# RWKV-7 hybrid block on one core: the product with the keys' norms ordered behind the fourth chunk's state update, with other places for the RWKV matmuls, the branch inputs and the output projection's first rounding

## The chip, the cores and the metric

The kernel runs on one core of a Trainium2 chip. A core has a matrix engine, TensorE (PE in the profile, its weight loads PEld), a vector engine (DVE), an activation engine (ACT), GpSimd (POOL) and SyncE (SP), whose work here is to issue DMA transfers. Each engine takes its instructions in an order fixed at compile time, and they wait for each other through semaphores. The metric is the device time of one execution in microseconds (us).

## What is computed

One decoder residual block over 512 positions of width 2048, in float32: an RWKV-7 time mixer and a sliding-window attention in parallel, both gated, projected and added to the input, then a gated convolutional feed-forward net.

```python
h = rms_norm(x, norm1_g);  z = h @ w_in
zs = token_shift(z[..., :RW_SHIFT_COLS], rw_mu)          # r, k, v and the low-rank inputs
o_rw  = rwkv7_mix(zs, ...);  o_att = swa_attention(q, k, v, ...)
g_rw, g_att = sigmoid(zg[..., :D_MODEL]), sigmoid(zg[..., D_MODEL:])
x = x + (g_rw * (o_rw @ w_branch[:RW_DIM]) + g_att * (o_att @ w_branch[RW_DIM:])) @ w_out
x = x + conv_ffn(rms_norm(x, norm2_g), w_up, conv_w, conv_b, w_down)
```

Inside the time mixer, with 16 heads of 64 channels:

```python
kk = k * k_k
kk = kk / max(sqrt(sum(kk * kk, per head)), 1e-12)        # the keys' norms
k  = k * (1 + (a - 1) * k_a)
# per position t:
sa    = state @ (-kk_t)
state = state * w_t + sa (x) (kk_t * a_t) + v_t (x) k_t
y_t   = state @ r_t
```

## The kernel before

**Precision.** Each float32 operand is split into a rounded high part (float32r, made on ACT) and a bfloat16 rest (made on DVE: value less high part); a product is three matmuls, high x high, high x low and low x high. `load_w` does this for a weight tile of 128 x 512: a DMA on SP's queue into `raw` (4 buffers), `whi` on ACT (L263), `wlo` on DVE (L264). `project` then issues 12 matmuls for each such tile (L284) and appends them to a list, `stream`.

**The stages.** Input projections for attention; the attention; the RWKV stage, in which the input projections of the gates run along; the branch projections (`w_branch`, again L284); the output projection `w_out` (L1107) and the feed-forward net (L1244, then L1107), each as a fast product of seven block products.

**The RWKV stage.** 16 heads are eight pairs `p`. `early(p)` projects k, r and v of the pair (three tiles of 48 matmuls), forms the decays and the keys' norms; `late(p)` does the recurrence in eight chunks of 64 positions. In the loop, `late(p)` is written down first, then a gate projection, `early(p + 1)`, and two more gate projections: six tiles, 288 stream matmuls for a pair. Pair `p` begins at stream index `base` = 960 + 288 p. So while the chunks of pair p run, the keys' norms of pair p + 1 are made.

**The keys' norms.** In `early`: `sq` on ACT (L642), sums on PE (L396), a reciprocal root of 13 small DVE instructions (`rq`, L198 to L207), and then `head_rows`: a transpose on PE (L399), a copy `rsT` on DVE (L401), a DMA from it to DRAM (`rsd`, L403) and two DMAs back that broadcast it over partitions (`rsb`, L407), all three on SP's queue. The product `kk = kk * rb` (L683, on DVE, kept in program order with the other instructions marked by `pin`) waits for them. Behind it come `kb = kk * ta` (L684, written into the tile `kz`), `bon` (L689, which doesn't need kk), and in the next `late` `BKK` (L699 from kb, L700 from k2) and `BAR` (L701 from kk, L702 from r), the operands of the first products L719.

**A chunk of `late`.** psG on PE (L848), GY on ACT (L851), psU on PE (L853), UV half on ACT (L855) and half on DVE (L856), psS on PE (L864), the state update SV of two DVE instructions (L870), then the next chunk's psG. After the fourth and the eighth chunk two DVE additions make `yc` (L876).

**What sets the order.** A scheduler at compile time orders the instructions of each engine by the order of writing and its own estimates, within the edges that the program gives. `behind(ins, before)` adds such an edge: `ins` is placed after `before`. It is an order, not a semaphore. With `held`, 34 or 35 matmuls of each pair are placed behind given stream matmuls: `entries` (the transposes, the levels of the triangular inverse, psG, psU and psS of the chunks) behind stream index `base + n + lag - 1`, n from the lists `LEVEL` and `CHUNK`. For psS of the eight chunks n is 175, 189, 203, 221, 235, 249, 263 and 277; a chunk's psU is four before it, its psG five before that (the first psG has no place). The transpose L399 has no such place.

**After the pairs.** `rin[i]` reads back the eight pairs' outputs from DRAM, and `split(rhi[:, i], ...)` rounds them on ACT and DVE for the branch projections; the last gate projections are written down between these roundings. Then `wp["step"]` and other counters set how often extra DRAM-to-DRAM sums are issued; they are not touched. In the output projection, `steps_of("o", i, ...)` fetches a tile `hraw` of the right operand and rounds it with `make()` (hhi on ACT, hlo on DVE, in `split`, L216 and L217); the first two are written after the branch projections but have buffers of their own, so the scheduler may place them earlier.

Of the kernel before, what the change touches and what calls it, by code (L numbers as in the profile page):

```python
# [13 lines left out]
AF = mybir.ActivationFunctionType  # L14
ALU = mybir.AluOpType
# [4 lines left out]
P = 128  # L20
S = 512
NT = S // P
# [113 lines left out]
def block_kernel(ctx: ExitStack, tc: tile.TileContext, d: Dims, a: dict, out: bass.AP):  # L136
    nc = tc.nc
    act, dve, pool, pe, sync = nc.scalar, nc.vector, nc.gpsimd, nc.tensor, nc.sync
    NK, NP, NQ, NKV, NF = d.NK, d.NP, d.NQ, d.NKV, d.NF
# [73 lines left out]
        return ins  # L213

    def split(hi, lo, src, pin=free):
        pin(act.activation(hi, src, AF.Copy))  # L216
        pin(dve.tensor_tensor(lo, src, hi.bitcast(F32) if hi.dtype == F32R else hi, op=ALU.subtract))  # L217


    def quarter(w, src, c):  # L220
# [31 lines left out]
    def behind(ins, before):  # L252
        tc.add_manual_dep(ins.ins, before.ins.name,
                          mybir.DependencyInfo(mybir.DependencyClass.NoSync, mybir.DependencyReason.DATA))

    def load_w(src):
        nk, ncol = src.shape[1:]
        n = nk * ncol
        raw = wp["raw"].tile([P, 512], F32, name="raw", tag="raw")[:, :n].rearrange("p (k c) -> p k c", c=ncol)
        wp["last"] = sync.dma_start(raw, src)  # L260
        hi = wp["hl"].tile([P, 512], F32R, name="whi", tag="whi")[:, :n].rearrange("p (k c) -> p k c", c=ncol)
        lo = wp["hl"].tile([P, 512], BF16, name="wlo", tag="wlo")[:, :n].rearrange("p (k c) -> p k c", c=ncol)
        act.activation(hi, raw, AF.Copy)  # L263
        dve.tensor_tensor(lo, raw, hi.bitcast(F32), op=ALU.subtract)  # L264
        wp["n"] += 1
        if wp["n"] in wp["after"]:
            wp["after"].pop(wp["n"])()
        elif wp["step"] == 3 and wp["n"] <= HELD:
            pass
        elif wp["n"] % wp["step"] == 0 or wp["n"] in extra:  # L270
            sums_along()()
        return hi, lo
# [23 lines left out]
    if True:  # L296
# [99 lines left out]
                pe.matmul(dst[:, t], sq[:, t * P : (t + 1) * P], K["sel2"], start=True, stop=True)  # L396

        def head_rows(pl, ps, rs, tag="lg", bufs=1):
            pe.transpose(ps[0 : 2 * NT, 0:P], rs, ident)  # L399
            sm = pl.tile([2 * NT, P], F32, name="rsT", tag="rsT", bufs=2)  # L400
            dve.tensor_copy(sm, ps[0 : 2 * NT, 0:P])  # L401
            rd = dram.tile([2 * NT, P], F32, name="rsd", tag="rsd", bufs=4)
            sync.dma_start(rd, sm)  # L403
            rb = pl.tile([P, S], F32, name="rsb", tag=tag, bufs=bufs)
            src = rd.rearrange("(h t) c -> h (t c)", h=2)
            for h in range(2):
                sync.dma_start(rb[h * HD : (h + 1) * HD], src[h : h + 1].to_broadcast([HD, S]))  # L407
            return rb
# [151 lines left out]
        with ExitStack() as pr:  # L560
# [21 lines left out]
            def bulk():  # L582
                return blk.tile([P, S], F32, name="bulk", tag="bulk")
# [41 lines left out]
            def r3(ap, c=C):  # L625
                return ap.rearrange("p (n c) -> p n c", c=c)

            def early(p):
                wl = lp.tile([P, 2 + NG, P], F32, name="wl", tag="wl", bufs=1)
                sync.dma_start(wl, a["lora"][p].rearrange("p (k c) -> p k c", c=P))  # L630
                w2 = wl[:, 0]
                ag = [lp.tile([P, NG, P], F32R, name=f"w{e}", tag=f"w{e}", bufs=2) for e in ("ghi", "glo")]
                split(*ag, wl[:, 2:])

                sums_along(up_jobs)()
                acc = ztile(d.c_k + p * P)
                kz = wtile("kz")
                shifted(acc, PR["mu"] + NP + p, kz, 0)
                kk = wtile("kk")
                dve.tensor_scalar(kk, kz, col("k_k", p), None, op0=ALU.mult)  # L640
                sq = wtile("lg")
                act.activation(sq, kk, AF.Square)  # L642
                ps = bulk()
                head_stats(ps, sq)
                rs = rsqrt_small(wk, ps[:, 0 : 2 * NT], None, None, mx=1e-24)
                rb = head_rows(wk, bulk(), rs, "lg")
                ps = bulk()
                for t in range(NT):
                    ts = slice(t * P, (t + 1) * P)
                    pe.matmul(ps[:, ts], thw[:, ts], w2, start=True, stop=True)  # L650
                lg = wtile("lw")
                act.activation(lg, ps, AF.Tanh, scale=0.5)
                dve.tensor_scalar(lg, lg, 1.0, None, op0=ALU.add)
                ps = bulk()
                for t in range(NT):
                    ts = slice(t * P, (t + 1) * P)
                    pe.matmul(ps[:, ts], lg[:, ts], K["tri"], start=True, stop=True)
                act.activation(Et[:, :, 1:], r3(ps), AF.Exp, scale=-0.5 * SQE)
                Ei = wtile("Ei")
                act.activation(Ei, ps, AF.Exp, scale=0.5 * SQE)  # L660

                ps = bulk()
                pe.matmul(ps, wl[:, 1], adz, start=True, stop=True)
                ta = wtile("at_")
                act.activation(ta, ps, AF.Tanh, scale=0.5, bias=half[:, 0, p : p + 1])

                acc = ztile(d.c_r + p * P)
                rz = wtile("rz")
                shifted(acc, PR["mu"] + p, rz, 1)
                acc = ztile(d.c_v + p * P)  # L670
                vz = wtile("vz", 2)
                shifted(acc, PR["mu"] + 2 * NP + p, vz, 0)

                k2 = wtile("k2")
                dve.tensor_scalar(k2, ta, half[:, 1, p : p + 1], half[:, 2, p : p + 1], op0=ALU.mult, op1=ALU.add)
                dve.tensor_tensor(k2, k2, kz, op=ALU.mult)
                dve.tensor_scalar(ta, ta, 0.5, 0.5, op0=ALU.mult, op1=ALU.add)
                kb = kz
                rk = wtile("lw")
                dve.scalar_tensor_tensor(rk, rz, col("r_k", p), k2, op0=ALU.mult, op1=ALU.mult)  # L680
                rkl = [wk.tile([P, S], F32R, name=f"rk{e}", tag="rhl" if e else "dd") for e in range(2)]
                split(*rkl, rk)
                pin(dve.tensor_tensor(kk, kk, rb, op=ALU.mult))  # L683
                dve.tensor_tensor(kb, kk, ta, op=ALU.mult)  # L684
                ps = bulk()
                for e in range(2):
                    pe.matmul(ps, bor, rkl[e], start=e == 0, stop=e == 1)
                bon = wtile("bon", 2)
                dve.tensor_tensor(bon, vz, ps, op=ALU.mult)  # L689
                return ag, Ei, kk, kb, k2, rz, vz, bon  # L690

            def late(p, st, norm, finish):
                ag, Ei, kk, kb, k2, rz, vz, bon = st
                Eex, Ein = Et[:, :, 0:C], Et[:, :, 1:]
                kb3, k23, Ei3, kk3, rz3 = (r3(x) for x in (kb, k2, Ei, kk, rz))
                for h, (lo, hi) in enumerate(HV):
# [148 lines left out]
                for n in range(NCH):  # L845
# [21 lines left out]
                            entries.append(ins)  # L867
                    if n < NCH - 1:
                        for h, (lo, hi) in enumerate(HV):
                            dve.scalar_tensor_tensor(SV[lo:hi, n + 1, h], SV[lo:hi, n, h], ee[lo:hi, n : n + 1],  # L870
                                                     s2[lo:hi, n % HN, h], op0=ALU.mult, op1=ALU.add)
                    if n % HN == HN - 1:
                        ns = slice(n + 1 - HN, n + 1)
                        for h in range(2):
# [38 lines left out]
                dve.tensor_tensor(yc, yc, ps, op=ALU.mult)  # L913
                pool.dma_start(o_rw_d[p], yc)

            entries, grams = [], []
            LEVEL = [36, 51, 64, 77, 89, 102, 116, 131, 144, 159]
            CHUNK = [171 + 14 * n + 4 * (n > 2) + x for n in range(NCH) for x in (-5, 0, 4)][1:]
            st, lt, held = early(0), None, []
            for p in range(NP):  # L920
                entries.clear()
                base = len(stream)
                lt = late(p, st, lambda done: lt and normed(lt, done), lambda: lt and final(p - 1, lt))
                emit_gate()
                if p + 1 < NP:
                    st = early(p + 1)
                sums_along(up_jobs)()
                for _ in range(GATES_PER_PAIR * NK // 16 - 1):
                    emit_gate()
                at = [31, *LEVEL[:8], *([137] if p else []), *LEVEL[8:], *CHUNK]  # L930
                lag = max(0, 8 - 4 * p)
                held += [(ins, base + n + lag - 1) for ins, n in zip(entries, at)]
                if p == 0:
                    held.append((grams[0], base + 11))
            entries.clear()
            normed(lt, None)
            final(NP - 1, lt)
# [7 lines left out]
        with tc.tile_pool(name="ain", bufs=1, side="right", reuse_waits="tile") as ainp:  # L945
# [9 lines left out]

            for i in range(NP):
                split(rhi[:, i], rlo[:, i], rin[i], pin)
                if i % 2:
                    emit_gate()
            while gates:  # L960
                emit_gate()
# [121 lines left out]
    def steps_of(w, i, acc, c, pl, got=None, flat=None):  # L1083
# [1 line left out]
        _, start, src, _, _ = PRODUCTS[i]  # L1085
        make, hhi, hlo = got or fetch(w, i, c, pl)
        if not got:
            make()
        for q in range(2):
            wr = raw_tile()  # L1090
            sync.dma_start(wr, quarter(w, src, c)[q])
# [530 lines left out]
```

## Time and profile before

| | us |
|---|---|
| median of 3 runs | 2703.35 |
| lowest and highest run | 2701.12, 2705.6 |
| the profiled execution | 2707.28 |
| its span, first to last instruction | 2705.4 |
| POOL busy | 458.0 |
| mean granted TensorE clock | 0.997 |

The profile is of one execution. Its page gives each engine's busy time, a picture of the span in 40 slices, the DMA queues, the chain of work that ended last and the costliest groups of instructions. A group reads: line, engine, operation, output<-inputs, shapes, count, then total and mean busy time and the idle time of the engine just before. Here are the first two groups, both of which appear below:

```profile
L1094 DVE TENSOR_TENSOR wlo<-raw,whi 128x1024 bf16<-128x1024 f32 x210 | 308.4, 1473 | 93.2 <-ACT whi L1093 92.5
L284 PE MATMUL acc<-xhi,whi 128*128 128x512 f32 x1152 | 348.8, 427 | 9.2 <-ACT whi L263 8.9
```

Other views of the same trace are used: the waits (who waited for whom, in total, how often, longest), the timeline (start, duration, engine, line, operation, operands; in brackets the idle time of the engine before it and what ended it), and windows (busy time of each engine in a stretch, with the clock that TensorE was granted, the mean busy share of the DMA engines and what they moved). A matmul's end is modelled, so a busy PE is not PE at its peak. SPq marks SP's queue of DMA issues.

### The profile page before, as it was taken

The page shows a single profiled execution, that of the slowest core. Times are in us where ns is not written, and L with a number is a line of the kernel's source. Part 1 is how long each engine was busy: PE and PEld are TensorE (multiplying, and loading weights), DVE is VectorE, ACT ScalarE, POOL GpSimd, SP SyncE. Part 2 cuts the span into 40 slices and gives each one's busy share as a digit, 9 for nine tenths or more (in the row PEclk, how much of TensorE's full clock was granted, in tenths as well). Part 3 has the DMA queues.
Part 4 walks back from the last instruction along what each step waited for, and adds up shares of the span by engine and source line. Part 5 has one row for each costly group of instructions (what it writes and reads, how often), then busy time and mean ns, then how long its engine had stood idle before and what let it go on. Part 6 is the DMA issues. An engine that isn't in the chain of part 4 may idle for free.

```text
span 2705.4 us, 46047 instructions
## 1 busy us (share of the span) xinstructions
PE 2663.3 (98%) x17426; PEld 1870.3 (69%) x17426; DVE 2053.8 (76%) x3387; ACT 1329.4 (49%) x2229; POOL 458.0 (17%) x455
## 2 busy tenths in 40 slices
PE   8999999999999999999999999999999999999999
PEld 5555566666666666555558999999999998555555
DVE  8787758767777874545678888888888888688887
ACT  6455435445544543322456555555555555444443
POOL 0001111011111001111000111111111110166665
PEclk9999999999999999999999999999999999999999
DMA  5566888788888777878785988988898888877885
GB/s 174 157 160 186 226 202 211 192 227 218 212 211 225 193 181 180 288 240 291 255 283 164 253 243 249 255 239 237 245 253 239 237 248 258 316 248 247 265 263 190
DMA packets 227759, 619.63 MB, mean 229 GB/s; under 512 B 24896, under 2 KB 45008, under 8 KB 227024
## 3 DMA queue, kind: packets, MB, share of 16 engines
q1 hardware_dynamic: 158976, 441.03, 49.6%
q0 software_dynamic: 37216, 136.33, 26.2%
q10 hardware_dynamic: 31344, 39.31, 4.2%
q8 instruction: 137, 2.24, 0.3%
q14 instruction: 86, 0.70, 0.1%
HBM read 566.96 MB, written 191.18 MB: 280 GB/s over the span
## 4 chain that ended last, share of the span: by engine, by line
PE 90%; DVE 5%; DMA 3%; issue 1%; ACT 1%; SPq 0%; DVEq 0%; ACTq 0%; POOL 0%; POOLq 0%
PE acc L284 29%; PE X L1244 18%; PE X L1107 11%; PE Y L1107 9%; PE Y L1244 9%; PE Z L1244 4%; PE psS L864 1%; PE psG L848 1%; DMA rsb<-rsd 1%; PE bulk L770 1%; PE bulk L719 1%; DVE wlo L264 1%; PE mi L549 1%; DMA raw<-in_w_z_dram 1%; PE bulk L786 1%
## 5 line engine op out<-in xcount | busy, mean ns | idle before, releaser
L1094 DVE TENSOR_TENSOR wlo<-raw,whi 128x1024 bf16<-128x1024 f32 x210 | 308.4, 1473 | 93.2 <-ACT whi L1093 92.5
L284 PE MATMUL acc<-xhi,whi 128*128 128x512 f32 x1152 | 348.8, 427 | 9.2 <-ACT whi L263 8.9
L263 ACT ACTIVATE whi<-raw 128x512 fp32r<-128x512 f32 x352 | 218.7, 627 | 278.0 <-PE acc L284 144.8
L1093 ACT ACTIVATE whi<-raw 128x1024 fp32r<-128x1024 f32 x210 | 214.9, 1053 | 274.5 <-POOL w L1098 158.5
L264 DVE TENSOR_TENSOR wlo<-raw,whi 128x512 bf16<-128x512 f32 x352 | 239.8, 688 | 139.1 <-ACT whi L263 118.0
L284 PE MATMUL acc<-xlo,whi 128*128 128x512 bf16 x1152 | 317.3, 382 | 0.0
L284 PE MATMUL acc<-xlo,wlo 128*128 128x512 bf16 x1072 | 292.3, 380 | 0.4 <-DVE wlo L264 0.4
L1244 PEld LDWEIGHTS <-wlo 128*128 128x128 bf16 x2464 | 237.6, 96 | 39.6 <-DVE wlo L1226 0.7
L1098 POOL COPY w<-whi 128x1024 bf16<-128x1024 bf16 x132 | 224.7, 1727 | 177.1 <-ACT whi L1093 177.1
L284 PEld LDWEIGHTS acc<-xhi,whi 128*128 128x128 f32 x1152 | 213.6, 191 | 58.5 <-ACT whi L263 9.4
L1244 PEld LDWEIGHTS <-whi 128*128 128x128 bf16 x2464 | 228.0, 98 | 33.1 <-issue 0.2
L284 PEld LDWEIGHTS <-wlo 128*128 128x128 bf16 x1408 | 137.6, 99 | 151.9 <-issue 9.0
L284 PEld LDWEIGHTS <-whi 128*128 128x128 bf16 x1408 | 126.5, 101 | 149.6 <-issue 48.1
L1226 DVE TENSOR_TENSOR wlo<-raw,whi 128x1024 bf16<-128x1024 f32 x184 | 224.2, 1220 | 6.2 <-ACT whi L1224 6.1
L1224 ACT ACTIVATE whi<-a 128x1024 fp32r<-128x1024 f32 x124 | 130.7, 1054 | 191.6 <-DVE a L1219 188.3
L1224 ACT ACTIVATE whi<-raw 128x1024 fp32r<-128x1024 f32 x184 | 193.1, 1051 | 41.7 <-issue 22.2
L1226 DVE TENSOR_TENSOR wlo<-a,whi 128x1024 bf16<-128x1024 f32 x124 | 151.9, 1225 | 72.0 <-ACT whi L1224 72.0
L243 POOL DMA_DIRECT2D s_dn<-in_w_dn_dram x88 | 72.7, 827 | 773.3 <-DMA s_dn<-s_dn 350.3
L1244 PE MATMUL X<-b,whi 128*128 128x256 f32 (+1 forms) x1472 | 195.2, 280 | 0.2 <-DVE x L1122 0.2
L1244 PE MATMUL Y<-t,whi 128*128 128x256 f32 (+1 forms) x1408 | 186.2, 280 | 0.0
L1244 PE MATMUL X<-t,whi 128*128 128x256 bf16 (+1 forms) x1408 | 185.4, 280 | 0.0
L1297 DVE SCALAR_TENSOR_TENSOR c<-u,par,c 128x512 f32<-128x512 f32 x176 | 131.7, 749 | 40.7 <-ACT c L1288 40.7
(396 smaller groups left out, 4718.4 us busy)
## 6 DMA issues: line engine op xcount, KB each, us to landing
raw<-in_w_up_dram SPq DMA_DIRECT2D x170, 512.0 KB, 5.3
raw<-in_w_z_dram SPq DMA_DIRECT2D x288, 256.0 KB, 5.1
s_dn<-in_w_dn_dram POOLq DMA_DIRECT2D x88, 512.0 KB, 7.0
raw<-s_dn SPq DMA_DIRECT2D x88, 512.0 KB, 4.3
raw<-in_w_up_dram POOLq DMA_DIRECT2D x80, 512.0 KB, 8.4
raw<-in_w_dn_dram SPq DMA_DIRECT2D x66, 512.0 KB, 4.4
s_dn<-in_w_dn_dram SPq DMA_DIRECT2D x44, 512.0 KB, 7.2
s_dn<-s_dn SPq DMA_DIRECT2D x44, 512.0 KB, 10.5
```

The lines of the kernel that those rows point to most:

```text
L243: return lambda: pool.dma_start(dst, second, accum_op=ALU.add, max_dma_last_dim=4096)
L263: act.activation(hi, raw, AF.Copy)
L264: dve.tensor_tensor(lo, raw, hi.bitcast(F32), op=ALU.subtract)
L284: stream.append(pe.matmul(acc, l, r, start=k0 + j == 0, stop=k0 + n == nk and j == len(ops) - 1))
L1093: act.activation(whi, wr, AF.Copy)
L1094: dve.tensor_tensor(wlo, wr, whi.bitcast(F32), op=ALU.subtract)
L1098: pool.tensor_copy(w16, top(whi))
L1107: pe.matmul(dst, l, r, start=fst and j == order[0], stop=lst and j == order[2], skip_group_check=True)
L1224: pin(act.activation(hi, t, AF.Copy))
L1226: return lambda: pin(dve.tensor_tensor(lo, t, hi.bitcast(F32), op=ALU.subtract))
L1244: pin(pe.matmul(ps, l, r, start=start and k == 0 and i == way[0], stop=k == KH - 1 and i == way[2], skip_group_check=True))
L1297: pin(dve.scalar_tensor_tensor(t, u[:, i, j + 1 : j + 1 + S], cw[:, j + 1, ci : ci + 1], t, op0=ALU.mult, op1=ALU.add))
```

## The change

The instructions stay the same, all of them; what changes is where some are placed.

- `early(p + 1)` gets `state`, the second half of pair p's fourth SV update, and places `kk = kk * rb` behind it.
- The transpose in `head_rows` (kept in `wp["turn"]`) is placed behind stream index `base + lag + 182`, for each pair that has a next one.
- `lag` was 8, 4, 0, 0, ... and becomes 10, 7, 4, 2, 0, ...; the first product of pair 0 (`grams[0]`) moves from 11 to 15.
- The gates between the roundings of the branch inputs come after the third, sixth and eighth, where they came after the second, fourth and sixth (three gates are left by then).
- The first two roundings of the output projection's right operand are placed behind the last `whi` of the branch projections.

```diff
     def split(hi, lo, src, pin=free):
-        pin(act.activation(hi, src, AF.Copy))
+        ins = pin(act.activation(hi, src, AF.Copy))
         pin(dve.tensor_tensor(lo, src, hi.bitcast(F32) if hi.dtype == F32R else hi, op=ALU.subtract))
+        return ins
...
-        act.activation(hi, raw, AF.Copy)
+        wp["whi"] = act.activation(hi, raw, AF.Copy)
...
         def head_rows(pl, ps, rs, tag="lg", bufs=1):
-            pe.transpose(ps[0 : 2 * NT, 0:P], rs, ident)
+            wp["turn"] = pe.transpose(ps[0 : 2 * NT, 0:P], rs, ident)
...
-            def early(p):
+            def early(p, state=None):
...
+                turn = wp["turn"]
...
-                pin(dve.tensor_tensor(kk, kk, rb, op=ALU.mult))
+                ins = pin(dve.tensor_tensor(kk, kk, rb, op=ALU.mult))
+                if state:
+                    behind(ins, state)
...
-                return ag, Ei, kk, kb, k2, rz, vz, bon
+                return ag, Ei, kk, kb, k2, rz, vz, bon, turn
...
                         for h, (lo, hi) in enumerate(HV):
-                            dve.scalar_tensor_tensor(SV[lo:hi, n + 1, h], SV[lo:hi, n, h], ee[lo:hi, n : n + 1],
-                                                     s2[lo:hi, n % HN, h], op0=ALU.mult, op1=ALU.add)
+                            ins = dve.scalar_tensor_tensor(SV[lo:hi, n + 1, h], SV[lo:hi, n, h], ee[lo:hi, n : n + 1],
+                                                           s2[lo:hi, n % HN, h], op0=ALU.mult, op1=ALU.add)
+                        states.append(ins)
...
-            entries, grams = [], []
+            entries, grams, states = [], [], []
...
+            LAG = [10, 7, 4, 2] + [0] * NP
...
-                    st = early(p + 1)
+                    st = early(p + 1, states[3])
...
-                lag = max(0, 8 - 4 * p)
+                lag = LAG[p]
                 held += [(ins, base + n + lag - 1) for ins, n in zip(entries, at)]
                 if p == 0:
-                    held.append((grams[0], base + 11))
+                    held.append((grams[0], base + 15))
+                if p + 1 < NP:
+                    held.append((st[-1], base + lag + 182))
...
                 split(rhi[:, i], rlo[:, i], rin[i], pin)
-                if i % 2:
+                if i % 3 == 2 or i == NP - 1:
                     emit_gate()
...
         if not got:
-            make()
+            ins = make()
+            if w == "o" and i == 0 and c < 2:
+                behind(ins, wp["whi"])
```

More of the change, by code (lines that the diff above doesn't have):

```diff
@@ L689, in early @@
                 dve.tensor_tensor(bon, vz, ps, op=ALU.mult)
-                return ag, Ei, kk, kb, k2, rz, vz, bon
+                return ag, Ei, kk, kb, k2, rz, vz, bon, turn
             def late(p, st, norm, finish):
-                ag, Ei, kk, kb, k2, rz, vz, bon = st
+                ag, Ei, kk, kb, k2, rz, vz, bon, _ = st
+                states.clear()
                 Eex, Ein = Et[:, :, 0:C], Et[:, :, 1:]
```

## The prediction

> **What bounds the kernel now.** I read the page's busy times first, then the waits of TensorE (PE), then the stretches in which those waits lie.
>
> ```profile
> PE 2663.3 (98%) x17426; PEld 1870.3 (69%) x17426; DVE 2053.8 (76%) x3387; ACT 1329.4 (49%) x2229; POOL 458.0 (17%) x455
> ```
>
> PE is busy for 2663.3 of 2705.4 us. An edit that only reorders can win PE's idle time, 42.1 us at most, and whatever a lowered clock stretched. So I asked the waits of PE alone, in 280 to 1070 us (the eight RWKV pairs) and in 1070 to 1500 us (the columns: who waits, on whom, total us, times, longest).
>
> ```profile
> PE psS L864 <- DVE UV L856: 14.0, 5, 5.7
> PE bulk L399 <- DVE rq L207: 3.3, 8, 0.5
> PE bulk L719 <- DVE bon L689: 0.6, 1, 0.6
> PE bulk L770 <- DVE XIW L810: 0.3, 1, 0.3
> PE bulk L770 <- DVE XIW L839: 0.3, 1, 0.3
> ...
> PE acc L284 <- ACT whi L263: 1.0, 1, 1.0
> ```
>
> One wait stands out: five times the state product psS waits for the copy UV on VectorE (DVE), up to 5.7 us. What is DVE doing then? Pair 0, in the timeline of DVE, SP and PE:
>
> ```profile
> 363.74 0.28 DVE L401 COPY rsT<-bulk 8x128 f32<-8x128 f32 x1
> ...
> 364.15 1.00 SPq L403 DMA_DIRECT2D rsd<-rsT  x1
> 372.02 1.11 SPq L407 DMA_DIRECT2D rsb<-rsd  x2
> ...
> 378.45 0.69 DVE L683 TENSOR_TENSOR kk<-kk,rsb 128x512 f32<-128x512 f32 x1 [5.82 <-DMA rsb<-rsd]
> ...
> 381.10 0.23 DVE L856 COPY UV<-psU 64x64 f32<-64x64 f32 x1
> ...
> 381.38 0.90 PE L864 MATMUL psS<-UV,W 128*128 128x64 f32 x3 [5.73 <-DVE UV L856]
> ```
>
> The keys' norms of the next pair leave as rsT at 363.74, go to DRAM and come back broadcast as rsb; the product kk stands in DVE's order before the third chunk's UV and waits 5.82 us for that round trip. The UV behind it needs nothing from kk; it is only queued. PE then idles 5.73 us.
>
> The stretches of the pairs, each from its first projection matmul to the next pair's (length; busy us of PE, PEld, DVE, ACT, POOL; clock; DMA share, GB/s), show the same:
>
> ```profile
> 306.04:410.11 104.07, 96.58 (x642) 64.17 (x641) 71.67 (x163) 43.86 (x96) 11.20 (x17) 0.97 0.82 209
> 410.11:510.26 100.15, 95.10 (x637) 62.92 (x636) 71.37 (x173) 45.49 (x99) 11.42 (x17) 0.97 0.80 199
> 510.26:604.12 93.86, 92.47 (x638) 61.30 (x636) 71.18 (x173) 45.08 (x99) 11.55 (x17) 1.00 0.86 222
> 604.12:699.73 95.61, 92.45 (x637) 61.27 (x636) 71.18 (x173) 45.09 (x99) 11.81 (x17) 1.00 0.84 216
> 699.73:793.26 93.53, 92.47 (x637) 61.25 (x636) 71.17 (x173) 45.07 (x99) 11.82 (x17) 1.00 0.86 220
> 793.26:886.01 92.75, 92.22 (x638) 61.34 (x636) 71.11 (x173) 45.08 (x99) 10.78 (x16) 1.00 0.83 211
> ```
>
> Pair 5 has no such wait and takes 92.75 us; with the same work pairs 1 to 4 take up to 7.40 us more. In pairs 0 and 1 the mean clock is 0.97 as well: after the long stalls PE runs slowly.
>
> ```profile
> 381.39:390.00 8.61, 8.61 (x34) 6.15 (x35) 5.94 (x13) 1.63 (x4) 0.72 (x3) 0.68 0.83 209
> 479.95:490.00 10.05, 10.05 (x41) 6.90 (x42) 7.07 (x15) 1.74 (x4) 1.42 (x3) 0.70 0.73 185
> ```
>
> **The change part by part.**
>
> *The product kk behind the fourth chunk's update, the transpose behind index 182 + lag.* No instruction is added. kk and what hangs on it move behind SV of chunk 4; the transpose that starts the round trip moves from where it stood, after 171 of the pair's projection matmuls, to behind the 183rd (index 182). Pair 5 gives the times after 171 and after 182 (L284 alone, busy and count):
>
> ```profile
> 793.26:844.43 51.17, 40.90 (x171) 20.89 (x171) 1.00 0.82 207
> 793.26:850.57 57.31, 43.72 (x182) 22.09 (x183) 1.00 0.82 211
> ```
>
> ```profile
> 845.27 0.28 DVE L401 COPY rsT<-bulk 8x128 f32<-8x128 f32 x1
> ...
> 855.40 0.68 DVE L683 TENSOR_TENSOR kk<-kk,rsb 128x512 f32<-128x512 f32 x1
> ...
> 863.67 0.59 DVE L870 SCALAR_TENSOR_TENSOR SV<-SV,ee,psS 64x64 f32<-64x64 f32 x2 [0.75 <-PE psS L864]
> 864.18 0.85 DVE L876 TENSOR_TENSOR yc<-GY,psS 64x256 f32<-64x256 f32 x2
> 865.35 0.69 DVE L264 TENSOR_TENSOR wlo<-raw,whi 128x512 bf16<-128x512 f32 x1 [0.32 <-ACT GY L851]
> 866.41 0.23 DVE L856 COPY UV<-psU 64x64 f32<-64x64 f32 x1 [0.37 <-ACT UV L855]
> ```
>
> So the transpose moves 6.4 us later (850.57 less 844.43, and one matmul of 0.24), rsT to 851.6, and kk gets its place after yc, at 865.03 at the earliest: 13.4 us for the round trip. What it needs, from rsT to kk's start, is 14.71 us in pair 0 (378.45 less 363.74) and at most 10.13 in pair 5, where kk did not wait. Pair 1 is as bad as pair 0:
>
> ```profile
> 463.49 0.28 DVE L401 COPY rsT<-bulk 8x128 f32<-8x128 f32 x1 [0.37 <-PE bulk L399]
> ...
> 478.33 0.69 DVE L683 TENSOR_TENSOR kk<-kk,rsb 128x512 f32<-128x512 f32 x1 [4.54 <-DMA rsb<-rsd]
> ```
>
> That is 14.84 us. I take the measured trips: in all pairs but 0 and 1 the norms are there in time, in those two kk still waits 1.3 and 1.4 us. Queued behind it is the fifth chunk's UV, for which psS on PE waits; UV needs to run at 866.41, kk would end at 867.1, so I charge 0.7 us each, 1.4 in all. Won: the 14.0 us of psS.
>
> The clock comes back with it. Over 8.61 us at 0.68 and 10.05 us at 0.70 PE lost 2.76 and 3.02 us: 5.8 us. [...]
>
> The transpose also stops waiting. Eight waits share the 3.3 us at L399; seven belong to the loop (the eighth, of pair 0's own keys, stays), and a place 6 us later is past the last step of the reciprocal roots on DVE. Won: seven eighths, 2.9 us. If the roots were to slide along on DVE, nothing.
>
> DVE's postponed work (kk, bon, kz and two BKK, five of 0.69, 3.4 us) now meets chunks 5 to 8. It fits: pair 5 has 71.11 us of DVE in 92.75. But a 0.69 us instruction ahead of a UV delays the chain; nothing in the trace shows this mix, the bounds are 0 and, with all five ahead of UV at 866.41 where 0.69 is free, 2.7 us in each of seven pairs. The nearest row is pair 5 itself, where kk and bon stood before a UV and PE lost nothing: I take 0.15, 1.0 in all.
>
> *The lags* (8, 4, 0, 0 become 10, 7, 4, 2; the first product 11 becomes 15). Later places give DVE time: the wait of 0.6 on bon goes (four matmuls at 0.24, 43.72 us over 182 in pair 5, are 1.0), and I count half of the two 0.3 at L770. Against it, pair 0's last chunk ends two matmuls later, 0.5 us, and pair 1's first products wait for the BAR written behind it:
>
> ```profile
> 405.92 0.69 DVE L702 TENSOR_TENSOR BAR<-rz,Et 64x512 f32<-64x512 f32 x1
> ...
> 406.85 3.62 PE L719 MATMUL bulk<-BAR,BKK 128*128 128x256 f32 x16
> ```
>
> The margin is 0.24 us (BAR ends at 406.61), so 0.3 us is lost. Net of the lags: 0.6 + 0.3 - 0.3 = 0.6, bounds -1 and 1.5.
>
> *Branch inputs.* The last gate projections now follow the third, sixth and eighth rounding, not the second, fourth and sixth, so a third rounding stands ahead of a gate's whi. The first two waited on ACT, and the counts of weight roundings (L263 on ACT) and of matmuls (L284 on PE and PEld) up to 1085.30 show PE's cushion:
>
> ```profile
> 1084.78 0.63 ACT L216 ACTIVATE rhi<-rin 128x512 fp32r<-128x512 f32 x1 [1.80 <-DMA rin<-o_rw_d]
> 1085.32 1.14 ACT L263 ACTIVATE whi<-raw 128x512 fp32r<-128x512 f32 x2
> ...
> 0.00:1085.30 1085.30, 175.45 (x281) 0.99 0.76 198
> 0.00:1085.30 1085.30, 828.91 (x3357) 414.48 (x3358) 0.99 0.76 198
> ```
>
> 281 rounded tiles serve 12 matmuls each, 3372; PE has started 3357: 15 matmuls, 3.6 us. A third input that comes 1.8 us after the second, as that one did, uses half of it. I cost it at nothing; without that cover up to 2 us.
>
> *The output projection's first rounding.* ACT stands 9.88 us before hhi, with a whi behind it for which PE waits 1.0 us:
>
> ```profile
> 1204.32 0.63 ACT L216 ACTIVATE hhi<-hraw 128x512 fp32r<-128x512 f32 x1 [9.88 <-DMA hraw<-h_o]
> ...
> 1204.86 0.61 ACT L263 ACTIVATE whi<-raw 128x512 fp32r<-128x512 f32 x1
> 1283.10 1.06 ACT L1093 ACTIVATE whi<-raw 128x1024 fp32r<-128x1024 f32 x1 [8.86 <-PE X L1107]
> ```
>
> Behind the last whi, hhi falls into the 8.86 us that ACT idles before 1283.10, two of 0.63. Won 1.0 us.
>
> *Sum.* 14.0 + 5.8 + 2.9 + 0.6 + 1.0 = 24.3, less 1.4 for kk and 1.0 for DVE's mix: 21.9 us. The profiled execution took 2707.28 us, 1.9 more than its span, and would come to 2685.4. It lies 3.9 above the median of the runs shown, 2703.35; from the median I predict **2681.4 us**. From 1500 us on PE follows its own chain, so nothing there eats the gain.
>
> **The rivals.**
>
> *The wait moves to the fifth chunk.* For it: two trips exceed 13.4 us, and a trip can change when it starts 6 us later among other transfers. Against: pair 5's, the nearest to a pair without stalls, leaves 3.3 us. If half of the psS stalls (7.0) and one clock loss (2.9) come back and DVE's mix costs 3.0, the gain is 24.3 - 12.9 = 11.4: 2692. [...]
>
> *Slower: the postponed block on DVE.* If all five instructions stand before the fifth UV, each pair pays 2.7 us, 19 in all, still a gain of about 5. It turns when rsb lands over 0.8 us after 865.03, that is a trip above 14.2 us, in every pair. At 16 us kk waits 2.6, each pair stalls 5.3 us, 37 in all, and if each lowers the clock, as the waits of 5.82 and 4.54 us did, 7 x 2.9 = 20 more: 57 - 24.3 = 33 slower, 2736. Against it: only the trips of pairs 0 and 1 were that long, and bon needs no kk and can run before.
>
> *The order isn't changed where it counts* (kk had its place late anyway, the transpose stays): 2703. Against: kk stands before the third UV in the rows above.
>
> **How the numbers follow.** Forecast (gain 18 to 28; 2675 to 2685) 0.62; wait moves (2685 to 2696) 0.25; slower block 0.06; no change or a gain below 5 us 0.07. A gain of 18 is the forecast with DVE's mix at 0.75 us a pair; 26 would be the forecast with nothing given back and every small wait of the pairs gone; two more allow for the spread of the runs shown (2701.12 to 2705.6). For 8 in 10 the range reaches from 2675 over most of the second case, to 2693. A measurement of this kernel tells 0.2%, 5.4 us, from no change. Faster: 0.62 + 0.25 and a little of the last, 0.88; same 0.06; slower 0.06.
>
> **What would show it.** Right: kk after the fourth SV in each pair, no idle before psS above 1 us, a clock of 1.00 in pairs 0 and 1, pairs 1 to 6 at 92.3 to 93.3 us, no wait at L399 but one, none before acc near 1200 us. Wrong: kk with a wait for rsb ahead of the fifth UV; waits of psS, psU or psG on SV, UV or GY in chunks 5 to 8; a first product L719 that waits for BAR; a whi that waits behind rhi.

## The result and the profile after

The changed kernel takes **2686.19 us** (median of 6 runs, 2685.23 to 2688.5); the kernel before, run beside it, 2704.88 us (median of 6, 2701.12 to 2708.59). The ratio is 0.9932, with a 95% interval of 0.9919 to 0.9945. The profiled execution of the changed kernel took 2686.41 us, its span is 2684.6 us.

Where the time went is best read from four stretches: up to pair 0's first projection matmul, pairs 0 to 6, the rest up to the first product of the output projection, and everything behind. First the windows view of before (length; busy us of PE, PEld, DVE, ACT, POOL with counts; clock; DMA share, GB/s):

```profile
0.00:306.04 306.04, 291.63 (x1408) 168.79 (x1408) 235.04 (x607) 161.10 (x364) 22.58 (x37) 1.00 0.64 177
306.04:978.74 672.70, 653.51 (x4452) 433.58 (x4451) 498.77 (x1195) 314.75 (x684) 78.46 (x115) 0.99 0.82 209
978.74:1281.05 302.31, 301.24 (x1563) 175.22 (x1561) 166.08 (x325) 102.89 (x195) 34.18 (x51) 1.00 0.79 239
1281.05:2705.40 1424.35, 1416.97 (x10009) 1092.75 (x10007) 1153.91 (x1262) 750.66 (x988) 322.80 (x252) 1.00 0.83 247
```

and the same view of the changed kernel:

```profile
0.00:306.69 306.69, 291.42 (x1408) 168.80 (x1409) 235.28 (x607) 161.49 (x364) 22.63 (x37) 1.00 0.64 177
306.69:958.86 652.17, 648.46 (x4452) 427.77 (x4451) 499.86 (x1195) 316.21 (x684) 78.13 (x115) 1.00 0.84 215
958.86:1259.94 301.08, 300.95 (x1562) 175.30 (x1561) 166.43 (x325) 103.21 (x195) 34.28 (x51) 1.00 0.80 241
1259.94:2684.60 1424.66, 1417.06 (x10009) 1092.80 (x10007) 1154.33 (x1262) 751.44 (x988) 324.15 (x252) 1.00 0.83 247
```

The pairs lost 20.53 us with the same 4452 matmuls. PE's idle time there fell from 19.19 us (672.70 less 653.51) to 3.71, which is 15.48; its busy time fell by 5.05, although no matmul went. Pairs 0 and 1, where the clock came back, account for 2.75 and 2.43 of that, the other pairs together for almost nothing. The columns lost 1.23 us; the first stretch grew by 0.65 and the last by 0.31. Together 20.80, the difference of the spans.

The waits of PE in the RWKV stage of the changed kernel (who waits, on whom, total us, times, longest):

```profile
PE bulk L397 <- ACT lg L643: 1.5, 1, 1.5
PE psS L869 <- DVE UV L861: 1.5, 4, 0.4
PE bulk L775 <- DVE XIW L844: 0.5, 2, 0.3
PE bulk L400 <- DVE rq L207: 0.3, 1, 0.3
```

The 14.0 us of psS are 1.5. All but one of the transpose's waits are gone (L400 is L399 of before). The wait at L397 lies in the start, before pair 0; it was 1.0 us in the profile of before and lies between under 0.2 and 1.6 in the kernels below. On DVE, pair 0 of the timeline now reads:

```profile
365.77 0.28 DVE L402 COPY rsT<-bulk 8x128 f32<-8x128 f32 x1 [1.77 <-PE bulk L400]
...
380.47 0.59 DVE L875 SCALAR_TENSOR_TENSOR SV<-SV,ee,psS 64x64 f32<-64x64 f32 x2
380.98 0.85 DVE L882 TENSOR_TENSOR yc<-GY,psS 64x256 f32<-64x256 f32 x2
381.75 0.68 DVE L685 TENSOR_TENSOR kk<-kk,rsb 128x512 f32<-128x512 f32 x1
...
383.90 0.23 DVE L861 COPY UV<-psU 64x64 f32<-64x64 f32 x1
```

kk starts behind yc with no idle time before it: the norms, which left as rsT 15.98 us earlier, have landed, and the next UV follows 2.15 us later. The pairs themselves (windows from first projection matmul to first projection matmul):

```profile
306.69:400.98 94.29, 93.83 (x642) 62.11 (x641) 71.63 (x163) 44.74 (x96) 11.01 (x16) 1.00 0.88 228
400.98:494.10 93.12, 92.67 (x638) 60.91 (x636) 71.74 (x173) 45.10 (x99) 11.58 (x17) 1.00 0.83 213
...
586.56:678.72 92.16, 91.82 (x638) 61.09 (x636) 71.30 (x173) 45.37 (x99) 11.68 (x17) 1.00 0.86 222
678.72:772.07 93.35, 92.69 (x637) 60.89 (x636) 71.29 (x173) 45.21 (x99) 11.62 (x17) 1.00 0.87 225
772.07:865.44 93.37, 92.71 (x637) 60.88 (x636) 71.30 (x173) 45.22 (x99) 10.77 (x16) 1.00 0.83 209
```

Pair 0 fell from 104.07 to 94.29 us, pair 1 from 100.15 to 93.12, both now at a clock of 1.00. Look also at the end of the list: pair 3, the last with a lag (2), takes 92.16 us, pairs 4 and 5 with lag 0 take 93.4, and pair 5 took 92.75 before. There the change gives something back, and there is something left to win.

### The profile page after: what moved, and what is told of

It reads as the page before. It is cut to its first block, busy times and chain, and to the rows that moved or that the text cites. A ratio compares the mean times of both kernels' runs of the same rounds, so it can differ in the third digit from the quotient of the medians.

```text
span 2684.6 us, 46031 instructions
## 1 busy us (share of the span) xinstructions
PE 2657.9 (99%) x17426; PEld 1864.7 (69%) x17426; DVE 2055.9 (77%) x3387; ACT 1332.3 (50%) x2229; POOL 459.2 (17%) x455
## 4 chain that ended last, share of the span: by engine, by line
PE 90%; DVE 4%; DMA 2%; issue 2%; ACT 1%; POOL 0%; ACTq 0%; SPq 0%; DVEq 0%; POOLq 0%
PE acc L285 29%; PE X L1255 18%; PE X L1118 11%; PE Y L1118 9%; PE Y L1255 9%; PE Z L1255 4%; PE psS L869 1%; PE psG L853 1%; PE bulk L724 1%; PE bulk L775 1%; DMA raw<-in_w_z_dram 1%; PE mi L550 1%; DVE wlo L265 1%; PE bulk L791 1%; PE scp L517 0%
## 5 line engine op out<-in xcount | busy, mean ns | idle before, releaser
L1105 DVE TENSOR_TENSOR wlo<-raw,whi 128x1024 bf16<-128x1024 f32 x210 | 307.8, 1470 | 92.3 <-ACT whi L1104 91.4
L1223 POOL DMA_DIRECT2D raw<-in_w_up_dram x80 | 69.8, 873 | 549.6 <-DMA raw<-in_w_up_dram 349.2
```

The source lines that it names most:

```text
L1105: dve.tensor_tensor(wlo, wr, whi.bitcast(F32), op=ALU.subtract)
L1223: pool.dma_start(w[n], a["w_up"][f, 1, int(n == "s1")], accum_op=ALU.add)
```

## The experiments

Eleven kernels: each part of the change undone or done alone, the lags taken further, and the distance from rsT to kk made shorter. Line numbers are those of each kernel itself; behind an edit they differ by a few from the changed kernel's. Times are medians with their range, the ratio is to the kernel before on the same chip. The changed kernel itself was not run beside them, so a difference from it is read from the ratios and the traces.

**kk alone.** The kernel before with nothing but the edge of kk.

```diff
...
-                pin(dve.tensor_tensor(kk, kk, rb, op=ALU.mult))
+                ins = pin(dve.tensor_tensor(kk, kk, rb, op=ALU.mult))
+                if state:
+                    behind(ins, state)
...
```

> The kernel before with kk placed behind the fourth state update and nothing else changed. Theory (kk's wait for rsb ahead of a UV was the cost): no idle of DVE before kk, no wait of psS on UV above 1 us, clock 1.00 in pairs 0 and 1, the eight waits at the transpose (3.3 us) still there; 14.0 + 5.8 us less than before, 2684 to 2689. Rival (the places, that is the lags and the transpose, make the gain and kk only follows): 2700 or more.

Measured: 2690.78 us (2689.06 to 2692.65, 4 runs), ratio 0.9947 (0.9927 to 0.9967). No wait of psS is left in the view, DVE never idles before kk, and the distance from rsT to kk is 18.5 us in pair 0 and 19.1 to 19.7 in the others. So this edge brings 0.53 of the 0.68 per cent by itself; the two intervals overlap, so how much the rest brings is read from the traces below. Among the waits of PE that it leaves:

```profile
PE bulk L400 <- DVE rq L207: 3.2, 7, 0.6
...
PE acc L285 <- DVE rlo L217: 1.3, 2, 1.1
PE X L1114 <- ACT whi L1100: 1.0, 1, 1.0
```

The last two (X at L1114 is L1118 of the changed kernel) are not in the profile of before, whose only wait in the columns is the 1.0 us of acc on whi. My reading is that they appear because the pairs end earlier and the old places of the branch inputs no longer fit; the experiment with the old gates bears on that.

**All but kk's edge.** The changed kernel without it.

```diff
-                    st = early(p + 1, states[3])
+                    st = early(p + 1)
```

> The changed kernel without the edge that puts kk behind the fourth update; all other places stay. By its order kk then stands between the third update and the fourth UV, and has some 10 us from rsT. Theory: trips of 10 to 15 us make DVE wait again for rsb, ahead of the fourth UV, 5 to 20 us in all with the clock; 2692 to 2706. Rival: within 2 us of the changed kernel, 2684 to 2688.

Measured: 2697.41 us (2687.81 to 2712.05, 10 runs), ratio 0.9974 (0.9954 to 0.9993). The waits of DVE and of PE in the pairs:

```profile
DVE kk L685 <- DMA rsb<-rsd: 11.9, 7, 3.9
```

```profile
PE psS L869 <- DVE UV L861: 11.8, 11, 3.9
```

kk stands before the fourth UV now (the later transpose pushed it one chunk on), waits in all seven pairs, and psS waits behind it. The median is 11 us above that of the changed kernel, and the 10 runs spread over 24 us, those of the changed kernel over 3.

**The transpose without a place.**

```diff
-                if p + 1 < NP:
-                    held.append((st[-1], base + lag + 182))
```

> The changed kernel without the place of the transpose. Theory: the 0.4 us waits at the transpose come back in seven pairs (2.9 us) while the waits of the first chunk's psS on UV (1.5 us in the changed kernel) go, so +0 to +2 us: 2685 to 2689, kk still without a wait. Rival (the place of the transpose is part of the gain, by 2.9 us or more): 2689 or more.

Measured: 2685.32 us (2684.48 to 2686.6, 4 runs), ratio 0.9927 (0.9908 to 0.9946): no different from the whole change.

```profile
PE bulk L400 <- DVE rq L207: 3.0, 7, 0.5
```

The seven waits of the transpose are back, 3.0 us, and the four of psS are gone. The place for the transpose wins 2.7 us and loses them again. Where it loses more than half of them shows in the changed kernel's pair 4, DVE first, then PE:

```profile
729.68 0.17 DVE L207 SCALAR_TENSOR_TENSOR rq<-rq,rq 128x8 f32<-128x8 f32 x1
729.77 0.69 DVE L265 TENSOR_TENSOR wlo<-raw,whi 128x512 bf16<-128x512 f32 x1
730.49 0.23 DVE L861 COPY UV<-psU 64x64 f32<-64x64 f32 x1
```

```profile
730.77 0.66 PE L869 MATMUL psS<-UV,W 128*128 128x64 f32 x4 [0.41 <-DVE UV L861]
```

Before, PE stood at the transpose until the roots `rq` were done; now it has no such halt and comes to psS while DVE is still at the same roots, with one wlo and the UV behind them.

**The old lags.** 8, 4, 0, 0, ... and the first product at 11.

```diff
-            LAG = [10, 7, 4, 2] + [0] * NP
+            LAG = [8, 4] + [0] * NP
...
-                    held.append((grams[0], base + 15))
+                    held.append((grams[0], base + 11))
```

> The changed kernel with the lags 8, 4, 0, 0 and the first product at 11 again. Theory: pairs 2 and 3 become as long as pairs 4 to 6 of the changed kernel (93.4 instead of 92.2 to 92.5 us), and the 0.6 us wait on bon returns: +1 to +4 us, 2687 to 2691. Rival (the lags carry a large part of the gain): 2694 or more.

Measured: 2689.34 us (2686.68 to 2690.0, 4 runs), ratio 0.9939 (0.992 to 0.9959).

```profile
PE psS L869 <- DVE UV L861: 2.3, 6, 0.5
PE bulk L724 <- DVE bon L693: 0.8, 1, 0.8
```

By the medians that is some 3 us more, by the ratios 2, and the two intervals overlap. The traces give 2.1: from one pair's first product to the next pair's, pairs 2 and 3 take 93.37 us each, where the changed kernel with its lags of 4 and 2 takes 92.47 and 92.15, and the spans differ by as much (2686.7 and 2684.6 us). The end of pair 1, with the larger lags and the later first product, comes at the same time in both (490.68 and 490.83 us). psS waits in six pairs, no longer in four. The wait on bon can't be laid to this edit: the kernels with lag 2, lag 4 and the free output rounding wait 0.6 to 0.8 us for bon with the new places, and the one with kk alone does not with the old ones.

**Lag 2 in the later pairs too.**

```diff
-            LAG = [10, 7, 4, 2] + [0] * NP
+            LAG = [10, 7, 4, 2] + [2] * NP
```

> The changed kernel with lag 2 in pairs 4 to 7 too (0 in the changed one). Theory (the lag gives DVE time in each pair): pairs 4 to 6 take 92.2 us, as pair 3 with lag 2 did, not 93.4, so 3 us less: 2682 to 2684. Rival (a step down of the lag to the next pair shortens a stretch, not the lag itself): pairs 4 and 5 stay at 93.3, 2685 to 2688.

Measured: **2680.26 us** (2679.31 to 2681.11, 4 runs) where before took 2704.88, ratio 0.9911 (0.9896 to 0.9925). All four runs lie below every run of the changed kernel (2685.23 us at the least, but not run beside it), though the intervals of the two ratios still touch. Pairs 3, 4 and 6, here from one pair's first product L724 to the next pair's (of PE's matmuls some records are missing, so only the lengths are used):

```profile
582.77:674.91 92.14, 91.14 (x625) 61.09 (x635) 71.48 (x173) 45.27 (x98) 11.56 (x17) 1.00 0.84 219
674.91:767.11 92.20, 91.13 (x625) 61.09 (x635) 71.44 (x172) 45.25 (x98) 11.87 (x17) 1.00 0.88 227
...
859.27:951.40 92.13, 91.13 (x626) 61.09 (x636) 71.27 (x172) 45.15 (x98) 9.92 (x15) 1.00 0.77 195
```

The last two take 1.2 us less than the 93.4 of lag 0, and pair 5 does too. So the 93.4 was no floor of PE. Why a later place helps is not shown: in the changed kernel PE is idle for 0.66 us in pair 4 and for 0.34 in pair 3, and the rest of the 1.2 lies in its busy time, whose ends are modelled. That the chunks' matmuls come to PE before DVE is through is my reading.

**Lag 2 and the transpose without a place.** The edits of the two experiments, lag 2 and no place for the transpose, together.

> As e5_lag2, without the place of the transpose. Theory: the transpose's place gives nothing (e3_turn_free), so within 1 us of e5_lag2: 2681 to 2684. Rival: with lag 2 the transpose's wait is real, 2.9 us more than e5_lag2.

Measured: 2681.85 us (2680.2 to 2683.28), ratio 0.9916 (0.9902 to 0.9931). No different from lag 2 alone: here too the transpose's place is worth nothing that these runs can tell.

**Lags 3 and 4.** Two kernels; the first as shown, the second with `[10, 7, 4, 4] + [4] * NP`.

```diff
-            LAG = [10, 7, 4, 2] + [0] * NP
+            LAG = [10, 7, 4, 3] + [3] * NP
```

> The changed kernel with lags 10, 7, 4, 3, 3, 3, 3, 3 (later places for the RWKV matmuls of all pairs). Theory (a pair whose matmuls stand two places later is free of DVE's delays, and then TensorE is simply full): nothing is left to win past a lag of 2; pairs 3 to 6 at 92.0 to 92.3 us, 2679 to 2682 us, as with a lag of 2. Rival (each further place still hides something): pairs below 91.8 us, 2674 to 2678 us. Third: the pair's last chunk ends later and the next pair's first products wait for BAR: pairs above 92.5, 2682 to 2686 us.

> The changed kernel with lags 10, 7, 4, 4, 4, 4, 4, 4. Theory: as with 3, 2679 to 2682 us. Rival (each further place still hides something): 2673 to 2678 us. Third (first products of the next pair wait for BAR, which is written behind the last chunk): a wait of 0.3 to 0.8 us of L724 on BAR in each pair, 2682 to 2688 us.

Measured: 2683.52 us (2682.56 to 2684.67, 4 runs), ratio 0.9931 (0.9916 to 0.9945), and 2682.33 us (2681.44 to 2685.46, 4 runs), ratio 0.9928 (0.9913 to 0.9943). No further gain, as the first theory had it, but the pairs are a little longer than with 2, which it did not have: pairs 3 to 6 take 92.53 to 92.56 us with lag 3 and 92.46 to 92.48 with lag 4, against 92.13 to 92.20. The times and, with lag 3, the pairs came out as in the third expectation, yet no wait of the first products on BAR shows in either trace, so its cause is not confirmed. With 4 another wait shows, XIW in every pair:

```profile
PE bulk L775 <- DVE XIW L844: 1.9, 7, 0.3
```

**The output projection's first rounding where it was.**

```diff
-            ins = make()
-            if w == "o" and i == 0 and c < 2:
-                behind(ins, wp["whi"])
+            make()
```

> The changed kernel without the edge of the output projection's first rounding. Theory: the wait of 1.0 us near 1200 us comes back and the 0.3 us at the first product of the output projection goes: +0.5 to +1 us, inside the noise of the times, seen in the waits. Rival (hidden anyway): no wait above 0.3 us there.

Measured: 2687.79 us (2684.95 to 2690.2), ratio 0.9938 (0.9923 to 0.9953). The wait of acc on whi returns, and the 0.3 us of X at L1118 goes. The time can't tell the two kernels apart, the trace can:

```profile
PE acc L285 <- ACT whi L264: 1.2, 1, 1.2
```

**The gates where they were**, behind the second, fourth and sixth rounding.

```diff
-                if i % 3 == 2 or i == NP - 1:
+                if i % 2:
```

> The changed kernel with the gates after each second rounding of the branch inputs. Theory (e1_kk_alone showed a wait of 1.3 us of the first branch product on rlo with this order): that wait shows again, +1 to +1.5 us. Rival (that wait came from e1's other places): no wait on rlo, 0 us.

Measured: 2687.52 us (2686.31 to 2691.93), ratio 0.9936 (0.9919 to 0.9953); the profiled execution has a span of 2690.2 us. Its waits in the columns, and the window behind the longer of them:

```profile
PE X L1118 <- ACT whi L1104: 2.5, 1, 2.5
PE acc L285 <- DVE rlo L217: 1.2, 2, 1.0
```

```profile
1275.00:1280.00 5.00, 4.73 (x14) 2.08 (x15) 3.79 (x4) 3.17 (x4) 0.00 (x0) 0.67 0.92 269
```

The branch inputs' rests `rlo` come 1.2 us late, the first products of the output projection 2.5, and the clock takes 1.7 us behind that (5.00 us at 0.67). This is the slowest of the four runs. The median is 1.3 us above that of the changed kernel, which the times can't tell from nothing; by this one trace the old places cost up to 5.

**The trip's threshold.** The transpose twenty places later, so that the distance between rsT and kk falls.

```diff
-                    held.append((st[-1], base + lag + 182))
+                    held.append((st[-1], base + lag + 202))
```

> The changed kernel with the transpose placed behind index 202 + lag instead of 182 + lag, kk where the change puts it (behind the fourth chunk's SV). Theory (what makes kk free in the changed kernel is the distance between rsT and kk, 16 to 17 us there against trips of up to about 15 us): twenty places at about 0.3 us take 6 to 7 us of it, so the distance without a wait would be about 10 us and every trip longer than that shows as idle time of DVE ahead of kk, 1 to 4 us in a pair, with the fifth chunk's UV and psS behind it; 2690 to 2705 us, pairs of 94 to 97 us where it waits. Rival (the gain comes from kk standing behind UV and SV, whatever the trip): no idle time before kk above 0.5 us, 2684 to 2688 us.

Measured: 2695.28 us (2686.61 to 2700.02, 8 runs), ratio 0.997 (0.9953 to 0.9986). In the profiled execution the distance is 9.5 to 10.1 us in five pairs, where the norms had landed in time; in two they had not, and DVE idled before kk for 7.8 us in all. Pair 2, first DVE, then PE, then the window behind:

```profile
558.37 0.28 DVE L402 COPY rsT<-bulk 8x128 f32<-8x128 f32 x1
...
573.76 0.69 DVE L685 TENSOR_TENSOR kk<-kk,rsb 128x512 f32<-128x512 f32 x1 [5.78 <-DMA rsb<-rsd]
```

```profile
575.96 1.12 PE L869 MATMUL psS<-UV,W 128*128 128x64 f32 x4 [5.57 <-DVE UV L861]
```

```profile
575.96:580.00 4.04, 4.04 (x14) 3.34 (x15) 3.48 (x7) 0.27 (x1) 0.80 (x1) 0.52 0.63 107
```

The trip took 15.39 us, the fifth chunk's psS stood for 5.57 and PE went on at 0.52. This is the rival in which the wait moves to the fifth chunk: the same order on DVE around kk, 6 to 7 us less distance. The runs spread over 13 us; that the trips differ from run to run is my reading, only one of the runs was profiled. I had expected waits of 1 to 4 us in more pairs; there were two, of 2.07 and 5.78.

## Why the prediction was right, and where its terms were off

The changed kernel was measured at 2686.19 us, inside the range of 2675 to 2693 and 4.8 above the 2681.4. It lies 1.2 above the 2675 to 2685 that I had given to the forecast itself, among the times of the rival in which the wait moves; the mechanism is the forecast's all the same, as its trace shows no wait of DVE before kk. Most of the 4.8 is one step: **the sum was made against the profiled execution and then taken from the median.** The sum gave 2685.4 us for an execution like the profiled one, and the profiled execution after took 2686.41; so the terms are off by 1.0 in all. The other 3.9 is the distance from the profiled execution of before to its median (less 0.2, by which the profiled execution after lies above its own). I took it for spread that every kernel shares. The runs say that it belonged to the very waits that were removed: the three kernels in which DVE waits for the norms spread over 13, 24 and 13 us (before in 13 runs; 7.5 in six), the ten others over 1.8 to 5.6, with four to six runs each. The trip to DRAM and back was over within 10.13 us in pair 5 of the kernel before (rsT at 845.27, kk at 855.40 without a wait) and took 15.39 in pair 2 with the later transpose, and only where something waits for it does the time follow. No trace of a faster run of before was kept, so this is read from the spreads alone. Where a profiled execution lies above the median because of waits that the change removes, the difference is no part of the gain at the median.

That the terms are off by only 1.0 is partly luck, as misses cancel. The pairs were to give 20.9 us and gave 20.53, and the columns 1.0 and gave 1.23; but inside the 20.9 a loss that was priced did not come and a gain that was priced did not either. The first stretch and the last, priced at nothing, grew by 0.96, with the wait at L397 0.5 us longer.

Term by term, with the profiles' numbers:

- *psS, 14.0, and the clock, 5.8*: right. kk alone shows the first, the windows of pairs 0 and 1 at 1.00 the second, with PE busy for 5.2 us less there. Pairs 1 to 6 were to take 92.3 to 93.3 us; they take 92.16 to 93.42.
- *kk's remaining wait, 1.4 lost*: none was measured. The distance from rsT to kk is 16 to 17 us, not 13.4. I had let the transpose move past the projection matmuls alone; three groups of the decays that followed it still follow it. The timeline of PE before, pair 5:

```profile
844.55 1.12 PE L650 MATMUL bulk<-wl,thw 128*128 128x128 f32 x8
...
846.82 1.16 PE L657 MATMUL bulk<-cst,lw 128*128 128x128 f32 x8
847.81 1.02 PE L663 MATMUL bulk<-adz,wl 128*128 128x512 f32 x2
```

  These 3.3 us stood between the transpose and index 182; they now stand between index 182 and kk. That is nearly all of what was missing, and with trips of up to 15.4 us it is what leaves the edge room: at a distance of 10 us the wait is back.
- *The transpose's waits, 2.9 won*: the waits went, the gain did not stay. psS of an early chunk meets the roots in their stead (1.5 us in four), and kk and its followers come later. Net nothing, by the kernel without that place. I had written the case down ("if the roots were to slide along on DVE, nothing"); what happened is that PE slid and the roots did not.
- *DVE's mix, 1.0 lost*: some 1.9, in the three pairs without a lag. Pairs 4 and 5 have the 637 and 638 matmuls that they had (of pair 5 the trace after has 637), and PE is busy for 92.69 and 92.71 us in place of 92.47 and 92.22, idle for 0.66 each: against the 92.75 us of pair 5 before that is 0.6 us a pair. In pairs 2 and 3, with lags of 4 and 2, nothing is lost. 0.3 of the 0.6 go with the transpose's place: without it these pairs take 93.07. What holds PE within its busy time wasn't taken apart.
- *Lags, 0.6 won*: too small, and for another reason than I gave; the old lags cost some 2 us, all of it in pairs 2 and 3. I had counted single waits, the one on bon first, and that one comes and goes whatever the lags. What a lag of 2 gives in this kernel is 1.2 us a pair, by a mechanism that the traces leave open.
- *Branch inputs, nothing*: their cover was computed from the old schedule, and went with it. Once the pairs are faster, the old places wait for `rlo` and for the first products of the output projection: 3.7 us of waits and 1.7 of clock in the one trace, 1.3 (within the spread) by the medians. The sum never saw that loss, because it appears only when the rest has been won.
- *The output projection's first rounding, 1.0 won*: right in kind, 0.7 net, as a wait of 0.3 us appears at the next tile.

Of the rivals, the wait that moves to the fifth chunk is real, as the later transpose shows, but begins at a shorter distance than this kernel has. The slower one would need trips above 16 us in every pair; the longest that a run shows is 15.39. That the order isn't changed is excluded by kk behind yc.

## What to carry to other kernels

If an instruction waits for a round trip through DRAM, don't ask what it needs but who is queued behind it on its engine, and place it so far down that the longest trip seen fits, not the mean one. Here the gain that came from such a wait took the wait's spread with it (7.5 us over six runs before, 3.3 after), and the profile that showed the wait long showed more than the median won (20.87 us between the two profiled executions, 18.69 between the medians of six). And cost the neighbours' cover in the new schedule: in the old one the branch inputs' rests `rlo` cost no wait, in the faster one, with the gates where they were, they are the next (1.2 us).

## What the hardware showed beside it

What the clock withheld behind a wait of PE came in two amounts in the windows read here, some 1.7 and some 3.4 us. Windows at the end of the two long stalls of psS in the kernel before:

```profile
380.00:390.00 10.00, 8.62 (x34) 6.16 (x35) 7.27 (x16) 1.63 (x4) 1.42 (x3) 0.66 0.72 180
475.00:490.00 15.00, 10.75 (x45) 7.00 (x43) 8.62 (x18) 1.74 (x4) 1.42 (x3) 0.77 0.79 211
```

and, in the kernel without kk's edge, behind its longest wait, 3.9 us, and a shorter one (PE is idle for 1.88 us of the second window):

```profile
475.00:485.00 10.00, 8.73 (x33) 6.40 (x34) 5.17 (x13) 1.60 (x4) 2.22 (x4) 0.66 0.99 232
665.00:675.00 10.00, 8.12 (x39) 5.64 (x39) 7.16 (x16) 2.08 (x5) 1.98 (x4) 0.83 0.73 184
```

The clock withheld 3.4 us three times (10.00 us at 0.66 twice, 15.00 at 0.77) and 1.7 once (10.00 at 0.83). What it withholds while PE still waits costs no time: in the kernel before it fell 1.2 and 0.8 us ahead of the end of the stalls, and the prediction's 2.76 and 3.02 us, read from there on, are what PE lost. There it stood at 0.50 for 6.8 us and then at 1.00 again:

```profile
380.20:387.00 6.80, 5.62 (x18) 4.39 (x19) 5.61 (x11) 0.90 (x2) 1.42 (x3) 0.50 0.66 122
479.20:486.00 6.80, 6.05 (x19) 4.38 (x20) 4.75 (x10) 0.90 (x2) 1.40 (x3) 0.50 0.64 132
387.00:390.00 3.00, 3.00 (x18) 1.77 (x17) 1.46 (x5) 0.74 (x2) 0.00 (x0) 1.00 0.89 323
486.00:490.00 4.00, 4.00 (x24) 2.52 (x23) 3.01 (x8) 0.85 (x2) 0.02 (x1) 1.00 0.82 274
```

At the start the kernel with kk alone waits 1.6 us for lg and then runs so:

```profile
285.00:290.00 5.00, 5.00 (x21) 3.75 (x19) 2.62 (x14) 1.11 (x2) 0.81 (x1) 0.66 0.97 288
```

Again 1.7 us, where the changed kernel waits 1.5 us at the same place and loses nothing (10.00 us at 1.00), and the kernel before lost nothing in pair 3 behind 2.64 us (15.00 at 1.00). With lag 3 the wait at that place is 1.3 us and the mean clock of the profiled execution 0.999, as with kk alone; the changed kernel has 1.000. The four waits of 3.9 us and more in the pairs were followed by the larger amount each (the fourth is the 5.57 us of the later transpose, with 7.90 us at 0.82 ahead of its end and 4.04 at 0.52 behind), those of 1.5 to 2.64 us by the smaller or none. What decides between the smaller one and none was not shown.

The trip of the norms, one write of 4.0 KB and two broadcast reads of 128.0 KB each, was over within 10.12 and 10.13 us in pairs 6 and 5 of the kernel before, took 11.17 to 14.84 us in the five pairs in which DVE waited for it there, and 15.39 in the later transpose's pair 2. SP's timeline of the changed kernel shows the first half of it:

```profile
366.08 0.29 SPq L404 DMA_DIRECT2D rsd<-rsT  x1
...
371.58 1.11 SPq L408 DMA_DIRECT2D rsb<-rsd  x2
```

5.5 us pass from the write's issue to that of the reads that wait for it; in the seven pairs of this kernel it is 3.7 to 7.8 us, in those of the kernel before 3.7 to 8.9. Where the traces give the reads' landing, it comes 3.0 to 3.4 us behind their issue in this kernel's pairs, 2.8 to 6.0 in those of the one before. How much of this is time behind other transfers is not shown: the DMA share is 0.75 to 0.88 in these pairs, and no run took the other transfers away.
